# Splitting the last 16 rows off two loads of a batched matmul, and moving one operand mix to VectorE

## The chip, the cores and the metric

One core of a Trainium2 chip. Times are device microseconds (us) of one execution. Medians come from three runs or more; ratios are over the fast runs of both kernels in the same rounds, so they are not quite the ratio of the medians quoted. The interval behind a ratio is its 95% interval.

## The reference

```python
# x, y: [8, 12, 512, 64] float32
def reference(x, y):
    return np.einsum('bhtc,bhsc->bhts', x, y).astype(np.float32)   # [8, 12, 512, 512]
```

96 independent products of 512x64 by 64x512. The inputs are 25.17 MB, the output 100.66 MB, so this is a problem of transfers.

## The kernel before

Heads are taken in 12 load groups of 8. x of a group is one transfer of 128 rows of 8 KB into the left half of a "slot" (128 partitions x 16 KB), y of the group another into its right half. The five slots also hold the outputs on their way out. All transfers are issued by SyncE into one queue. `P` = 128, `Q` = 16, `R` = 32, `C` = 64, `NG` = 12, `SLOTS` = 5.

```python
    def slot():
        return slots.tile([P, K * S], fp32, name="slot")

    def load(g):
        both = slot()
        nc.sync.dma_start(both[:, :R * C], xv[g])
        nc.sync.dma_start(both[:, R * C:], yv[g])
        loaded[g] = both

    def compress(g):                  # float32 -> bf16; frees the slot
        both = loaded.pop(g)
        xk = kept.tile([P, R, C], bf16)
        nc.scalar.activation(xk..., both[:, :R * C], COPY)          # all of x, ScalarE
        ...
        # y in quarters: partitions 0-63 on VectorE and GpSimd (yb0),
        #                partitions 64-127 on VectorE and ScalarE (yb1)

    def mix(i, engines, halves=(0, 1)):    # xk into the zeroed operand tile, four copies
        ...

    def result(o):
        ...                                # matmuls into PSUM, two copies into a slot
        if h == 0 and i + 2 < 2 * NG:
            transposes(i + 2)
        elif h == 1 and FIRST <= i + 4 < 2 * NG:
            mix(i + 4, [nc.scalar if o % 4 == 3 else nc.vector] * 4)
        return lambda: nc.sync.dma_start(ov[i, h], otf)              # 2 MB store

    with tc.manual_schedule():
        for g in range(SLOTS):
            load(g)
        for half, engine, part in ((0, nc.vector, 256), (1, nc.gpsimd, 64)):
            for k in range(0, K * E * D, part):
                engine.memset(zeroed[half][:, k:k + part], 0.0)
        stores = []
        for g in range(NG):
            compress(g)
            mix(g // 2, [nc.gpsimd] * 4, (g % 2,))
            if g in (2, 4):
                transposes(g // 2 - 1)
            if g < 5:
                load(g + SLOTS)
            elif g in (5, 7, 9):
                stores.append(result(len(stores)))
            elif g in (6, 8):
                load(g // 2 + 7)
        ...
```

Below, x3 is the x load of group 3, y10 the y load of group 10. The slots go round: x5 can be issued when group 0 has been converted, the first output takes group 5's slot, and the last pair (x11, y11) takes group 8's.

## Time and profile before

| | before |
|---|---|
| time, median (lowest to highest) | 301.92 us (301.58 to 302.05, 5 runs) |
| span of the profiled run | 300.3 us |
| x0 landed, first to last of its 16 parts | 5.32 to 5.65 us |
| y2 landed | 17.73 to 18.05 us |
| x11 issued / landed | 54.19 / 59.98 to 60.29 us |
| last store's last part | 299.42 us |

One more row of the same page, what the transfers moved in each of the 40 slices (7.5 us each):

```profile
GB/s 282 430 422 421 420 423 422 421 432 443 420 432 438 417 434 437 421 437 434 420 437 434 423 432 432 423 443 426 421 450 419 426 439 423 419 437 428 426 434 194
```

From the second slice to the last but one the rate stays between 417 and 450 GB/s. Nothing that is lost in the queue of transfers can be won back later.

### The profile page before, as it was taken

What the parts mean: (1) busy time and instruction counts of PE and PEld (TensorE: products, weight loads), DVE (VectorE), ACT (ScalarE), POOL (GpSimd) and SP (SyncE); (2) the same over time, 40 slices, a digit from 0 to 9 for tenths busy, and PEclk for the clock granted to TensorE, in tenths of its full rate; (3) what the DMA queues carried; (4) which work ended last, traced back from release to release, by engine and by line L of the source; (5) the groups of instructions that cost most, each with busy time, mean ns of one, the idle gap of its engine ahead of it and who ended that gap; (6) DMA issues with size and microseconds to landing.
All of it is one profiled execution on the core that took longest, in us unless ns stands there. A gap on an engine that the chain in (4) does not pass through costs nothing.

```text
span 300.3 us, 1359 instructions
## 1 busy us (share of the span) xinstructions
PE 143.4 (48%) x384; PEld 46.3 (15%) x384; DVE 180.8 (60%) x136; ACT 219.2 (73%) x133; POOL 59.3 (20%) x56
## 2 busy tenths in 40 slices
PE   0004044037547674656675557664665675674000
PEld 0001011012212121211221112121221221121000
DVE  1568895969794973947909649289195552503200
ACT  4666599996999969789788697887887977364000
POOL 2899999991000000000000000000000000000000
PEclk9999995676998769767657866759667758577555
DMA  7999999999999999999999999999999999999994
GB/s 282 430 422 421 420 423 422 421 432 443 420 432 438 417 434 437 421 437 434 420 437 434 423 432 432 423 443 426 421 450 419 426 439 423 419 437 428 426 434 194
DMA packets 10375, 125.92 MB, mean 419 GB/s; under 512 B 1152, under 2 KB 1152, under 8 KB 1152
## 3 DMA queue, kind: packets, MB, share of 16 engines
q1 hardware_dynamic: 10368, 125.83, 98.8%
q8 instruction: 3, 0.05, 0.1%
q14 instruction: 4, 0.03, 0.0%
HBM read 25.17 MB, written 100.66 MB: 419 GB/s over the span
## 4 chain that ended last, share of the span: by engine, by line
DMA 49%; ACT 13%; DVE 5%; issue 4%; PE 1%; DVEq 1%; ACTq 0%
DMA out_dram<-slot 49%; ACT slot L65 10%; DVE slot L67 4%; ACT xb L65 2%; PE pm L134 1%; DVEq L191 1%; ACT xk L82 1%; DVE yb L67 0%; ACT yb L65 0%; DVE yT L120 0%; DVEq L67 0%; ACTq L65 0%
## 5 line engine op out<-in xcount | busy, mean ns | idle before, releaser
L134 PE MATMUL pm<-yT,xT 128*128 128x512 bf16 x384 | 143.4, 519 | 132.5 <-ACT slot L65 78.1
L65 ACT ACTIVATE slot<-pm 128x2048 f32<-128x2048 f32 x72 | 131.1, 1876 | 40.0 <-DMA out_dram<-slot 31.6
L67 DVE COPY slot<-pm 128x2048 f32<-128x2048 f32 x24 | 53.8, 2285 | 70.3 <-DMA out_dram<-slot 49.0
L134 PEld LDWEIGHTS <-xT 128*128 128x128 bf16 x384 | 46.3, 121 | 228.6 <-issue 192.6
L115 DVE STREAM_TRANSPOSE xT<-xb 128x1024 uint32<-128x1024 uint32 x24 | 49.1, 2044 | 8.4 <-PE pm L134 7.0
L65 ACT ACTIVATE xb<-xk 32x1024 bf16<-32x1024 bf16 x36 | 48.1, 1337 | 0.8
L67 DVE CAST yb<-slot 64x1024 bf16<-64x1024 f32 x24 | 32.7, 1362 | 19.0 <-DMA slot<-in_y_dram 18.7
L67 POOL COPY xb<-xk 32x1024 bf16<-32x1024 bf16 x24 | 38.1, 1589 | 1.2
L82 ACT ACTIVATE xk<-slot 128x2048 bf16<-128x2048 f32 x12 | 22.9, 1910 | 9.6 <-DMA slot<-in_x_dram 9.5
L67 DVE COPY xb<-xk 32x1024 bf16<-32x1024 bf16 x36 | 26.1, 725 | 0.4
L120 DVE STREAM_TRANSPOSE yT<-yb 128x512 uint32<-128x512 uint32 x24 | 25.2, 1048 | 0.0
L67 POOL CAST yb<-slot 64x1024 bf16<-64x1024 f32 x12 | 19.8, 1653 | 7.4 <-DMA slot<-in_y_dram 6.8
L65 ACT ACTIVATE yb<-slot 64x1024 bf16<-64x1024 f32 x12 | 15.9, 1328 | 3.6 <-DMA slot<-in_y_dram 3.4
L82 ACT ACT_TABLE_LOAD x1 | 1.3, 1283 | 0.7 <-PEq L180 0.7
L149 DVE MEMSET xb<- 128x256 uint32 x4 | 1.1, 272 | 0.9 <-PEq L180 0.9
L149 POOL MEMSET xb<- 128x64 uint32 x16 | 1.4, 152 | 0.3 <-POOLq L180 0.3
L180 POOL MEMSET const-float32-0.0<- 128x1 f32 x1 | 0.1, 98 | 0.2 <-issue 0.2
L180 POOL MEMSET const-float32-1.0<- 128x1 f32 x1 | 0.1, 98 | 0.0
L180 POOL MEMSET const-bfloat16-1.0<- 128x1 bf16 x1 | 0.1, 98 | 0.0
L180 POOL MEMSET const-uint8-127<- 128x1 uint8 x1 | 0.1, 98 | 0.0
## 6 DMA issues: line engine op xcount, KB each, us to landing
out_dram<-slot SPq DMA_DIRECT2D x48, 2048.0 KB, 20.5
slot<-in_x_dram SPq DMA_DIRECT2D x12, 1024.0 KB, 17.6
slot<-in_y_dram SPq DMA_DIRECT2D x12, 1024.0 KB, 19.3
```

The lines of the kernel that those rows point to most:

```text
L65: nc.scalar.activation(dst, src, COPY)
L67: engine.tensor_copy(dst, src)
L82: nc.scalar.activation(xk.rearrange("p r c -> p (r c)"), both[:, :R * C], COPY)
L115: nc.vector.transpose(xT.rearrange("p (k r e) -> p k e r", k=K, e=E), xb.rearrange("p (k e c) -> p k e c", k=K, e=E),)
L120: nc.vector.transpose(yT.rearrange("p (r j) -> p j r", r=D), yb.rearrange("p (j c) -> p j c", c=D))
L134: nc.tensor.matmul(pm[:, j, :], xT[:, k + j, h, :], yT[:, h * S:(h + 1) * S], start=True, stop=True)
L149: engine.memset(zeroed[half][:, k:k + part], 0.0)
L180: nc = _bacc.Bacc("TRN2", target_bir_lowering=False, num_devices=1)
L191: with _tile.TileContext(nc) as tc:
```

## The change

The intent, as far as the diff tells it: the 16 transfer engines don't end together (the last store's parts land over 3 us), so work is shifted between them. Of x0 and y2, only 112 rows go as one transfer; the last 16 rows go as four transfers of 4 rows, one behind each of the loads that follow. Two smaller edits: the last mix goes from ScalarE to VectorE, and a memset is done in one piece.

```diff
+    loaded, inputs, mixed, made, later = {}, {}, {}, {}, []
     def load(g):
+
         both = slot()
-        nc.sync.dma_start(both[:, :R * C], xv[g])
-        nc.sync.dma_start(both[:, R * C:], yv[g])
+        for src, dst, apart in ((xv[g], both[:, :R * C], g == 0), (yv[g], both[:, R * C:], g == 2)):
+            rows = P - Q if apart else P
+            nc.sync.dma_start(dst[:rows], src[:rows])
+            later.extend((dst[k:k + 4], src[k:k + 4]) for k in range(rows, P, 4))
+            if later:
+                nc.sync.dma_start(*later.pop(0))
         loaded[g] = both
@@ result
-            mix(i + 4, [nc.scalar if o % 4 == 3 else nc.vector] * 4)
+            mix(i + 4, [nc.scalar if o % 4 == 3 and i + 5 < 2 * NG else nc.vector] * 4)
@@ schedule
-        for half, engine, part in ((0, nc.vector, 256), (1, nc.gpsimd, 64)):
+        for half, engine, part in ((0, nc.vector, 1024), (1, nc.gpsimd, 64)):
```

The queue then holds, in order (s is a transfer of 4 rows): x0 (112 rows), s, y0, s, x1, s, y1, s, x2, y2 (112 rows), s, x3, s, y3, s, x4, s, y4, and so on with whole loads. x0 is complete with the fourth s, y2 with the eighth.

More of the change, by code (lines that the diff above doesn't have):

```diff
@@ L56 @@
     pmpool = ctx.enter_context(tc.tile_pool(name="pmpsum", bufs=2, space=bass.MemoryType.PSUM))
-    loaded, inputs, mixed, made = {}, {}, {}, {}
+    loaded, inputs, mixed, made, later = {}, {}, {}, {}, []
     zeroed = [const.tile([P, K * E * D], u32, name=f"xb{half}") for half in range(2)]
```

## The prediction

> **What bounds the kernel now.** I read the page from its second part down. First the row of the 40 slices, to see whether one resource is full all the time:
>
> ```profile
> PE   0004044037547674656675557664665675674000
> DVE  1568895969794973947909649289195552503200
> ACT  4666599996999969789788697887887977364000
> POOL 2899999991000000000000000000000000000000
> DMA  7999999999999999999999999999999999999994
> ...
> HBM read 25.17 MB, written 100.66 MB: 419 GB/s over the span
> ```
>
> The transfers are at 90% or more in every slice but the first and the last. No compute engine is full for long, except GpSimd (POOL) in the first quarter. The split by stage, cut where the loads end (62.7 us), says the same; its last two columns are the share of the transfer engines and GB/s:
>
> ```profile
> 57.50:62.70 5.20, 3.26 (x8) 1.04 (x8) 3.04 (x3) 5.16 (x3) 5.03 (x4) 0.54 1.03 427
> 62.70:150.00 87.30, 50.57 (x148) 16.87 (x147) 67.04 (x52) 75.94 (x48) 5.32 (x4) 0.78 1.01 431
> 150.00:296.00 146.00, 79.21 (x206) 25.08 (x204) 71.56 (x51) 97.11 (x59) 0.00 (x0) 0.67 1.01 429
> ```
>
> So the end is set by the queue of transfers: it must never run empty, and its 16 engines should end together. Two numbers come from the trace's record of when each of a transfer's 16 parts landed. The first load's parts land at 5.32 to 5.65 us, the eighth's at 22.70 to 23.03: 2.48 us a load of 128 rows, so **0.31 us a row** on each engine (8 rows). And the last store's parts land at 296.21 to 296.71 (twelve), 297.2, 297.2, 297.85 and **299.42**: one transfer engine ends 1.6 us after the next and 3 us after most. That is what the change seems to aim at.
>
> Then the early timeline, since there the change acts (start, length, engine, line, what; in brackets the idle time before it):
>
> ```profile
> 5.68 1.91 ACT L82 ACTIVATE xk<-slot 128x2048 bf16<-128x2048 f32 x1 [3.66 <-DMA slot<-in_x_dram]
> ...
> 10.09 3.07 POOL L67 COPY xb<-xk 32x1024 bf16<-32x1024 bf16 x2
> ...
> 20.58 2.02 DVE L115 STREAM_TRANSPOSE xT<-xb 128x1024 uint32<-128x1024 uint32 x1
> ...
> 33.25 3.52 DVE L67 CAST yb<-slot 64x1024 bf16<-64x1024 f32 x2
> ...
> 36.89 3.65 ACT L65 ACTIVATE slot<-pm 128x2048 f32<-128x2048 f32 x2 [2.58 <-DVE yb L67]
> ...
> 50.86 1.91 ACT L82 ACTIVATE xk<-slot 128x2048 bf16<-128x2048 f32 x1
> 52.80 1.32 ACT L65 ACTIVATE yb<-slot 64x1024 bf16<-64x1024 f32 x1
> ...
> 54.19 0.33 SPq L74 DMA_DIRECT2D slot<-in_x_dram  x1
> ```
>
> The reader is to see a chain: the first output copy (36.89) waits until VectorE has read y of load group 5, since it takes that group's buffer. From it ScalarE runs in order, without a gap worth naming, to its read of y of group 8 (ends 54.12), and only then is the last x load issued (54.19), into group 8's buffer. That load lands at 60.29, straight behind the one before it (57.79), so the queue never ran dry. How much slack is there? The first load, which found the queue empty, landed 4.9 us after issue (0.74 to 5.65). Issued at 54.19 onto an empty queue the last x load would have landed at 59.1. **The slack is 1.2 us.**
>
> [...] The trace before has only 128-row loads, each landing in 16 parts[...] all 24 loads land in the order of issue, 2.48 us apart. [...] One engine here moves 8 KB in 0.31 us, about 26 GB/s[...].
>
> **The change, part by part.**
>
> Rows moved: the two thinned loads lose 16 rows each, 1 row per engine and load if evenly, so all engines save 2 rows (0.62 us)[...] That is the whole gain on offer.
>
> When x of group 0 is complete: its last 4 rows stand behind y of group 1, the fourth load, which landed at 12.76 to 13.09. [...] 7+1+8+1+8+1+8+1 = 35 rows in place of 32, so it is 3 x 0.31 = 0.93 later: about **14.0 us, not 5.65**. The order of instructions shows the waits for these rows ahead of ScalarE's table load (1.28 us), so the first conversion of x runs from 15.2 to 17.1 and GpSimd's first pair of copies starts there instead of at 10.09. GpSimd is then 7 us late, with about 4.8 us of work per group against 4.97 us per group of loads: it recovers almost nothing.
>
> When y of group 2 is complete: its last 4 rows stand behind x of group 4, the ninth load (25.18 to 25.51). [...] 78 rows there in place of 72: 6 x 0.31 = 1.86 later, **27.4 us, not 18.05**. Its lower 64 partitions are needed by VectorE and GpSimd only from the 112 rows, so GpSimd is not held again; but VectorE's and ScalarE's casts of the upper half wait, and both run in order.
>
> VectorE from 27.4, with the durations of before: second half of y2 1.24 (28.6); the transpose pair 2.8 (31.4); y3 2.5 (33.9); y4 2.5 (36.4); the next transpose pair 2.8 (39.2; GpSimd's copies for it end near 34.8); y5 2.5 to 3.5 (about **42.2**; before 36.77). The first output copy on ScalarE starts there. Before, from that copy to the issue of the last x load it was 54.19 - 36.89 = 17.3 us, all ScalarE's own work in order; I keep it. VectorE's casts of y7, needed for the second output copy, end near 52.3 (GpSimd to 44.5, transposes 2.8, two groups of casts 5.0), just in time for 52.5. So the last x load is issued at 42.2 + 17.3 = **59.5**, and lands at 59.5 + 4.9 = 64.4 instead of 60.29. **The queue runs empty and the loads end 4.1 us later.** After it the stores have their lead back: the fourth store can be issued near 74.3 and is due only near 81, so nothing is added. Nor is it won back, as the queue is full from there to the end. The empty queue also lines the engines up again: [...] so the 0.62 us gain is lost.
>
> The last x mix: four ScalarE copies of 1.337 us (5.3) become four of VectorE's 0.725 us (2.9), late in the store phase where both have idle time: 0. One memset of 1024 columns for four of 256 (0.272 each, 1.1 in all): 0, since it ends long before the first y lands. Eight more issues on SyncE at some 0.33 to 0.65 us each fit under 2.5 us of transfer per load: 0.
>
> Sum: 301.92 + 4.1 = **306.0 us**.
>
> **The rivals.** (a) The balancing works and no hole opens: 301.92 - 0.6 = 301.3. For it: the 3 us of imbalance at the end, and a change so particular that its author may have measured it. Against it: 1.2 us of slack against a delay of 5.3 us. [...] (b) [...] a small transfer takes 4 to 5 row times, 1.2 to 1.5 us instead of 0.31, [...] some 8 us more at y of group 2. VectorE's chain moves with it, and the last x load, with earlier ones, comes about 9 us later still: 306 + 9 = 315. [...] partial overlap would give 308 to 311. (c) ScalarE or GpSimd becomes the bound for good: GpSimd has work only to 68 us, and later stores have leads of 20 us from issue to landing, so no.
>
> **Range and chances.** I give (a) a quarter, the hole alone (303 to 308) a little over a third, (b) in part or in full the rest. Two per cent slower is 308.0, so slower gets 0.41, same 0.58; a gain of over 2% (below 295.9) is under the transfers' own time, 0.01. The range 300.9 to 315.0 covers (a) to nearly all of (b).
>
> **What would show it.** Right: the first conversion of x starts near 15 us; the casts of y of group 2 end near 29; the last x load is issued near 59.5; the slices of the transfers show a dip near 57 to 62 us with ScalarE's wait or SyncE's wait on ScalarE's y cast ahead of it. Wrong: no dip and the last load landing near 60 (then (a)); or small transfers that land over a microsecond after the load ahead of them, and dips already near 38 us (then (b)).

## The result, and the profile after

The changed kernel took **317.72 us** (317.39 to 318.39, 5 runs) against 301.92: ratio 1.0531 [1.0516, 1.0545], slower. 306.0 and a range of 300.9 to 315.0 had been predicted. The profiled spans differ by 16.0 us (316.3 against 300.3).

The page of the changed kernel, its second and third part (tenths of busy time in 40 slices of 7.9 us, then the rate):

```profile
DVE  1312299995998767296592955919569195501400
ACT  0065294999799997896988878888788547285000
POOL 1229699993600000000000000000000000000000
...
DMA  7999999959999999999999999999999999999995
GB/s 218 334 258 314 335 423 421 400 218 311 431 429 430 432 431 431 431 429 430 431 431 431 431 431 425 431 431 431 431 433 429 431 431 429 423 433 427 431 429 222
...
HBM read 25.17 MB, written 100.66 MB: 398 GB/s over the span
```

The row of busy transfers shows one dip, in the ninth slice. The row of rates shows two losses: slices 2 to 5 (7.9 to 39.5 us) run at 258 to 335 GB/s **while the engines count as busy**, and slices 8 to 10 hold the dip. The same in a split by stage; the last two columns are the share of the transfer engines and GB/s. Before:

```profile
3.00:28.00 25.00, 3.57 (x8) 1.24 (x9) 13.60 (x10) 14.85 (x9) 19.16 (x12) 1.00 1.01 424
57.00:80.00 23.00, 11.86 (x35) 4.03 (x35) 19.05 (x16) 20.25 (x13) 10.85 (x7) 0.74 1.02 432
```

After, and a second split of it around the dip:

```profile
3.00:28.00 25.00, 0.00 (x0) 0.00 (x0) 5.76 (x5) 9.66 (x6) 8.13 (x6) 1.00 1.01 298
57.00:80.00 23.00, 8.98 (x20) 2.65 (x19) 19.22 (x13) 22.62 (x14) 16.90 (x12) 0.50 0.81 304
```

```profile
69.00:71.40 2.40, 0.00 (x0) 0.00 (x0) 2.37 (x2) 2.35 (x3) 2.14 (x2) 0.50 0.01 3
```

From 3 to 28 us the share is 1.01 in both kernels, but the rate is 298 in place of 424 GB/s. So in this trace the share doesn't tell the loss and the rate does: an engine whose row is held up (the next table has rows of up to 1299 ns) counts as busy. From 69.0 to 71.4 us the queue was truly empty (3 GB/s).

What the rows themselves took, from the trace's record of each row's transfer, 3.3 to 28 us, 8 KB rows only:

| kernel | rows over 350 ns | rows over 700 ns, number | longest |
|---|---|---|---|
| before | 0.1% | 0 | 460 ns |
| after | 45% | 82 | 1299 ns |

It begins with the 112 rows of x0 by themselves: of the rows that started between 3.3 and 5.2 us, before any part of a small transfer had landed (the first at 6.58), 65 of 69 took over 350 ns, against 1 of 99 in the kernel before. The 112 rows of y2 (21.0 to 24.0 us) had a median of 572 ns a row, where a row took 0.31 us before. And between 9.1 and 10.45 us, around the second small transfer, **all 16 engines** had a row of 0.78 us or more (the trace names no engine, but 16 such rows are in flight at once from 9.75 to 9.95 us).

The timeline of the changed kernel (start, length, engine, line, what; in brackets the idle time before it), to be read beside the prediction's:

```profile
18.20 1.28 ACT L87 ACT_TABLE_LOAD   x1 [18.20 <-DMA slot<-in_x_dram]
19.49 1.91 ACT L87 ACTIVATE xk<-slot 128x2048 bf16<-128x2048 f32 x1
...
21.46 2.68 POOL L67 COPY xb<-xk 32x1024 bf16<-32x1024 bf16 x2 [8.98 <-ACT xk L87]
...
37.25 1.33 ACT L65 ACTIVATE yb<-slot 64x1024 bf16<-64x1024 f32 x1 [9.28 <-DMA slot<-in_y_dram]
37.25 0.72 DVE L67 CAST yb<-slot 64x1024 bf16<-64x1024 f32 x1 [9.89 <-DMA slot<-in_y_dram]
...
49.49 3.54 DVE L67 CAST yb<-slot 64x1024 bf16<-64x1024 f32 x2
...
53.15 3.65 ACT L65 ACTIVATE slot<-pm 128x2048 f32<-128x2048 f32 x2 [4.69 <-DVE yb L67]
...
69.05 1.33 ACT L65 ACTIVATE yb<-slot 64x1024 bf16<-64x1024 f32 x1
...
70.44 0.33 SPq L77 DMA_DIRECT2D slot<-in_x_dram  x1
...
79.41 2.49 DVE L67 CAST yb<-slot 64x1024 bf16<-64x1024 f32 x2 [3.58 <-DMA slot<-in_y_dram]
```

The first conversion of x starts at 19.49 and not at 5.68; VectorE and ScalarE wait 9.9 and 9.3 us for the last rows of y2; the first output copy starts at 53.15 and not at 36.89; x11 is issued at 70.44 and not at 54.19.

Where the 16 us were lost is told by the landing times of the last loads (last of the 16 parts, from the trace's own record):

| | before | after | later by | added in this step |
|---|---|---|---|---|
| y10 (22nd load) | 57.79 | 69.03 | 11.24 | 11.24 |
| x11 (behind the dip) | 60.29 | 75.34 | 15.05 | 3.81 |
| y11 | 63.35 | 79.38 | 16.03 | 0.98 |
| last store | 299.42 | 315.43 | 16.01 | -0.02 |

So 11.2 us were lost in the slow stretch, 3.8 in the empty queue, and 1.0 at the hand-over from loads to stores. Of y10's parts twelve are 9.8 to 10.0 us late and four 11.2 (as many as the parts of a small transfer); six more rows on these four, at 0.31 us (the prediction's estimate: 78 rows in place of 72), are 1.9 of these 11.2, and the rest is slow rows. The stores took the same time in both. The last store's parts again land in the pattern of before: twelve at 312.46 to 312.92, then 313.88, 314.14, 314.39 and 315.43. Nothing was balanced.

### The profile page after: what moved, and what is told of

It reads as the page before. It is cut to its first block, busy times and chain, and to the rows that moved or that the text cites.

```text
span 316.3 us, 1370 instructions
## 1 busy us (share of the span) xinstructions
PE 143.4 (45%) x384; PEld 46.2 (15%) x384; DVE 186.6 (59%) x137; ACT 214.1 (68%) x129; POOL 56.4 (18%) x56
## 4 chain that ended last, share of the span: by engine, by line
DMA 44%; ACT 15%; DVE 4%; issue 4%; PE 3%; DVEq 1%; ACTq 0%
DMA out_dram<-slot 44%; ACT slot L65 12%; DVE slot L67 4%; PE pm L139 3%; ACT xb L65 1%; ACT yb L65 1%; DVEq L196 1%; ACT xk L87 1%; DVE yb L67 0%; DVE yT L125 0%; DVEq L67 0%; ACTq L65 0%
## 5 line engine op out<-in xcount | busy, mean ns | idle before, releaser
L67 DVE CAST yb<-slot 64x1024 bf16<-64x1024 f32 x24 | 35.5, 1480 | 33.4 <-DMA slot<-in_y_dram 33.1
L65 ACT ACTIVATE xb<-xk 32x1024 bf16<-32x1024 bf16 x32 | 42.8, 1337 | 0.7
L67 POOL COPY xb<-xk 32x1024 bf16<-32x1024 bf16 x24 | 37.2, 1551 | 11.0 <-ACT xk L87 9.0
L67 DVE COPY xb<-xk 32x1024 bf16<-32x1024 bf16 x40 | 29.0, 726 | 0.4
L65 ACT ACTIVATE yb<-slot 64x1024 bf16<-64x1024 f32 x12 | 15.9, 1329 | 9.6 <-DMA slot<-in_y_dram 9.3
L67 POOL CAST yb<-slot 64x1024 bf16<-64x1024 f32 x12 | 17.8, 1487 | 16.5 <-DMA slot<-in_y_dram 16.0
L154 DVE MEMSET xb<- 128x1024 uint32 x1 | 0.9, 912 | 1.0 <-PEq L185 1.0
```

The costliest lines, as they stand in the source:

```text
L65: nc.scalar.activation(dst, src, COPY)
L67: engine.tensor_copy(dst, src)
```

## The experiments

Three theories stood at first. **PLACE**: whether rows collide, that is, hold up each other and the rows of the loads, depends on the partitions that they go to; rows of neighbouring ones do (an assumption). **COUNT**: a transfer of few rows costs its time wherever it goes. **LATE**: the cost is that rows arrive late, behind other loads. The figures that the expectations of e2, e4, e5, e6 and e10 give first are those of PLACE. In each case the time is that of the run named, against 301.7 to 302.0 for the kernel before on the same chip.

### 1. The two other edits alone (e1)

The changed kernel with whole loads; the memset and the last mix stay changed.

```diff
-        for src, dst, apart in (...):          # the split
-            ...
+        nc.sync.dma_start(both[:, :R * C], xv[g])
+        nc.sync.dma_start(both[:, R * C:], yv[g])
```

> The changed kernel with its loads put back whole (128 rows, no 4-row transfers); the single memset and VectorE's last x mix stay. All theories: the loads alone are to blame, so 301.9 us within 0.5 of the kernel before. If the other two edits cost or gain anything, it shows here.

Measured: 302.18 us, ratio 1.0009 [0.9994, 1.0024]. The two edits are worth nothing; all 15.8 us come from the split loads.

### 2. The same 16 rows in one piece (e6), and the small ones straight behind their load (e7)

```diff
 e6:
-            later.extend(...)
-            if later:
-                nc.sync.dma_start(*later.pop(0))
+            if apart:
+                nc.sync.dma_start(dst[rows:], src[rows:])
 e7:
-            if later:
+            while later:
                 nc.sync.dma_start(*later.pop(0))
```

> The changed kernel, but the last 16 rows of x 0 and y 2 go in one 16-row transfer straight behind the 112 rows: no 4-row transfers, no late completion. [...] rows of the 112-row transfers still collide ([...]0.45 to 0.65 us a row), and the 16 rows[...] take about 1.1 us; together 5 to 6 us of stall, about 307 us unless slack hides it nowhere, as the queue is always full. Rival (only the 4-row transfers and the lateness are to blame): 302 us.

> The changed kernel, but the four small transfers stand straight behind their 112 rows, so x 0 is complete near 11 us and y 2 near 26 us counted with all collisions before it. All collisions stay, the lateness goes. If the two causes add (collisions delay the loads by about 10 us, lateness adds the empty queue of about 5 us): 311.5 us, with no empty stretch before the last x load. If lateness is no cause of its own: 317.7 us.

Measured: e6 306.09 us (1.0138 [1.0123, 1.0153]); e7 311.36 us (1.0315 [1.0291, 1.0339]). Both close to what was expected (some 307 and 311.5). In both, x0 and y2 are completed right behind their 112 rows (e7: y2 at 28.59 us, against 37.23 in the changed kernel), so little of LATE is left. The splits by stage, e6 and then e7:

```profile
3.00:28.00 25.00, 0.26 (x1) 0.21 (x2) 10.54 (x9) 13.20 (x9) 14.74 (x10) 1.00 1.01 356
```

```profile
3.00:28.00 25.00, 0.00 (x0) 0.00 (x0) 5.62 (x5) 9.67 (x6) 12.73 (x8) 1.00 1.02 283
57.00:80.00 23.00, 7.31 (x17) 2.25 (x17) 16.04 (x13) 20.68 (x13) 20.27 (x13) 0.50 0.98 383
```

e7 has the slow stretch of the changed kernel (283 GB/s) but hardly its dip: the share from 57 to 80 us is 0.98 in place of 0.81. By the medians, and roughly, slow transfers cost 311.36 - 301.96 = 9.4 us, and having the rows behind later loads 317.72 - 311.36 = 6.4. The cut costs 4 us even when its 16 rows go in one piece (e6).

### 3. Extra small transfers beside whole loads (e4, e5, e10)

To have the small transfers by themselves: the kernel before, with eight extra transfers of 4 rows x 5.6 KB into a tile that nobody reads, at the places in the queue where the changed kernel has them. e4 takes four neighbouring partitions of 96 to 127; e5 takes partitions 4 apart, 16 in a span, from the same region; e10 takes partitions 0, 4, 8, 12 and so on from 0 to 15 and 32 to 47. In the changed kernel each small transfer landed in four parts; by estimate, eight of them here give four of the engines eight short rows more each.

```diff
+    spare = const.tile([P, 1408], fp32, name="spare")
+    # later: at eight places, which partitions
+    #   e4:  lo + 4*j .. lo + 4*j + 3      with lo = 112, then 96
+    #   e5:  lo + j, +4, +8, +12           with lo = 112, then 96
+    #   e10: lo + j, +4, +8, +12           with lo = 0, then 32
+            if (g, which) in later:
+                some = later[g, which]
+                nc.sync.dma_start(spare[some], src[g][some, :1408])
```

> The kernel before, all loads whole, plus eight extra 4-row transfers (5.6 KB a row, 4 neighbouring partitions each) into an unused tile, behind the loads where the change has its own. No 112-row transfer, nothing completes late. [...] each holds up all engines for some 0.5 to 0.7 us (four rows[...] at 0.21 us a row alone), so the tenth load lands 4 to 5.5 us late and the time is 305 to 308 us. Rival: small neighbouring transfers are harmless without the 112-row ones or the lateness: 302 to 303 us.

> The same, with the extra transfers' rows 4 partitions apart. [...] the tenth load lands 1 to 2.5 us late and the time is 302 to 304.5 us, clearly under the run with neighbouring rows. Rival COUNT (fixed cost per transfer): the same as with neighbouring rows.

> The eight extra 4-row transfers again, into partitions 0, 4, 8, 12 and their like[...] no row of the first 10 loads takes longer than 0.35 us; [...] 8 x 0.21 = 1.7 us more, the others nothing; if the engine that ends last is not among them, 302.0 us, else 303.6. Rival COUNT (each small transfer stalls all engines, wherever its rows go): 305.5 us, as with the other two placings.

| | time, ratio [95%] | rows over 350 ns / number over 700 ns | y10 landed, first to last part (before: 57.49 to 57.79) |
|---|---|---|---|
| e4 | 306.38, 1.0137 [1.0114, 1.0161] | 18% / 48 | 61.14 to 62.85 |
| e5 | 305.48, 1.0118 [1.0101, 1.0134] | 20% / 7 | 59.52 to 62.11 |
| e10 | 303.43, 1.0056 [1.0039, 1.0073] | 0.2% / 0 | 57.59 to 59.37 |

The splits by stage of e4, e5 and e10:

```profile
3.00:28.00 25.00, 1.92 (x5) 0.80 (x6) 11.23 (x10) 12.64 (x8) 15.49 (x10) 1.00 1.01 369
```

```profile
3.00:28.00 25.00, 1.81 (x5) 0.80 (x6) 11.56 (x10) 12.94 (x8) 15.82 (x10) 1.00 1.01 389
```

```profile
3.00:28.00 25.00, 3.57 (x8) 1.24 (x9) 12.70 (x10) 14.07 (x9) 18.16 (x12) 1.00 1.01 424
```

The same eight transfers, the same bytes at the same places in the queue: with four neighbours of 96 to 127 the first part of y10 is 3.65 us late, in e10 0.1 us. So **COUNT falls**: the number of transfers and their size are the same, and which rows they take decides. PLACE fits. Why those rows and not others was not shown: the trace names no engine and not which partition a row goes to, and the rows that are read from HBM changed together with the partitions that are written, so a cause on the reading side was not ruled out. e5 misses its expectation of 302 to 304.5 us: its rows, 4 apart in the region of e4, leave 20% of the rows over 350 ns (e4 18%), though fewer over 700 ns (7 against 48), and the times of e4 and e5 are not clear of each other. e10's rows are 4 apart as well, and 0.2% are over 350 ns. So it is not the distance between the rows by itself that decides.

One thing more stands in these traces: the small rows themselves took 0.22 us in all three kernels. The slow ones are 8 KB rows of the loads, and in e4 210 of the 224 slow rows between 3.3 and 40 us started within 1 us after a small row.

In e10 twelve engines are 0.1 us late at y10 and four 1.6 us, close to 8 x 0.22 us for rows of 5.6 KB. The cost of 4-row transfers that I had predicted is thus right for the rows of e10. e10 still loses 1.6 us by the medians; the first parts of x11 are 0.15 us late and those of y11 1.35, so nearly all of it comes between these two. See experiment 6.

### 4. The split rows of the real loads, 4 apart (e2)

```diff
-            later.extend((dst[k:k + 4], src[k:k + 4]) for k in range(rows, P, 4))
+            later.extend((dst[k:P:4], src[k:P:4]) for k in range(rows, rows + (4 if apart else 0)))
```

> The changed kernel, but each 4-row transfer takes rows 4 apart (112+j, 116+j, 120+j, 124+j) in place of 4 neighbouring ones: same count, size, order, waits. [...] rows of the small transfers take 0.31 to 0.65 us in place of 1.1, only the two 112-row transfers stay slow (some 4 us together) and the late completion of x 0 and y 2 stays; about 309 us, range 305 to 312. Rival COUNT (a transfer on 4 engines costs a fixed stall whatever its rows): unchanged, 317.7 us.

Measured: 314.26 us (313.36 to 315.28), 1.041 [1.0377, 1.0442]. Outside the expected 305 to 312, between the two expectations: spreading the rows wins 3.5 of 15.8 us. That is in line with e5, where rows 4 apart left 7 rows over 700 ns against 48 in e4, though about as many over 350 ns (20% against 18%). The 112-row part, which e6 shows to be slow as well (y2's rows took a median of 468 ns there, in place of 310), is unchanged.

### 5. Late whole loads, nothing split (e3, e8, e9)

The kernel before, with only the order of the first ten loads changed. e8 has y2 ninth, e9 has x0 fourth, e3 both.

```diff
-            load(g)
+            loaded[g] = slot()
+        # e3: y0 x1 y1 x0 x2 x3 y3 x4 y2 y4
+        # e8: x0 y0 x1 y1 x2 x3 y3 x4 y2 y4
+        # e9: y0 x1 y1 x0 x2 y2 x3 y3 x4 y4
+        for g, which in (...):
+            load_one(g, which)
```

> The kernel before with whole loads, but issued in another order: x of group 0 fourth, y of group 2 ninth. No small and no 112-row transfer, only the late completion (x 0 lands near 13.1 us, y 2 near 25.5). Theory LATE (my predicted chain): VectorE's casts of y 5 end near 41.1 in place of 36.8, the last x load is issued near 58.4 and lands near 63.3 in place of 60.3: 304.9 us. If lateness is harmless (all the loss is in the transfers themselves): 301.9 us.

> Whole loads, x 0 first as in the kernel before, y of group 2 ninth. By my chain the lateness of y 2 drives VectorE's order and with it the last x load: nearly all of the 6.9 us that both late loads cost, 307 to 309 us. If the lateness of x 0 (GpSimd's start) is what counts: 302 to 303 us.

> Whole loads, x of group 0 fourth (lands near 13.1 us), y of group 2 in its usual turn. As y 2 alone cost 6.9 us, and both together no more, x 0 alone should cost nothing that y 2 did not hide: VectorE's first transposes wait for GpSimd by a microsecond or two at most and the last x load has 1.2 us of slack: 302 to 303.5 us. Rival (any late first load empties the queue later): 305 us or more.

| | time, ratio [95%] | first output copy | x11 issued | x11 / y11 landed, against before |
|---|---|---|---|---|
| before | 301.92 | 36.89 | 54.19 | |
| e9 (x0 late) | 304.79, 1.0098 [1.0083, 1.0113] | 38.89 | 57.39 | +1.88 / +2.92 |
| e8 (y2 late) | 308.79, 1.0227 [1.0211, 1.0242] | 44.16 | 61.45 | +5.90 / +6.89 |
| e3 (both) | 308.84, 1.0232 [1.0215, 1.025] | 44.21 | 61.52 | +6.00 / +6.95 |

Here no row is slow in the first 50 us (from 3.3 to 28 us at most 3 of some 1280 rows over 350 ns); the split by stage of e3:

```profile
3.00:28.00 25.00, 0.00 (x0) 0.00 (x0) 6.36 (x6) 10.84 (x7) 10.59 (x8) 1.00 1.01 424
```

424 GB/s, as before, and yet 6.9 us are lost: 6.0 by the time x11 lands, and 1.0 behind it. Of the 6.0, 0.9 are there when y10 lands, as x10 was issued at 51.20 in place of 43.88; the rest is an empty queue ahead of x11. The row of rates of e8 shows the gap in its seventh to ninth slice:

```profile
GB/s 292 427 421 424 419 424 375 224 265 434 435 419 440 424 427 438 423 438 431 424 438 433 425 433 427 433 431 425 440 429 427 435 427 431 425 429 431 431 425 226
```

So LATE is a true cost of its own. e8 came as expected (307 to 309), but e3 missed its 304.9: right in kind, and 3.9 us too small. e8's timeline shows part of the reason:

```profile
25.46 2.48 DVE L67 CAST yb<-slot 64x1024 bf16<-64x1024 f32 x2 [9.96 <-DMA slot<-in_y_dram]
...
30.70 7.07 DVE L67 CAST yb<-slot 64x1024 bf16<-64x1024 f32 x4
...
31.93 3.51 POOL L67 COPY xb<-xk 32x1024 bf16<-32x1024 bf16 x2
...
40.52 3.52 DVE L67 CAST yb<-slot 64x1024 bf16<-64x1024 f32 x2
...
44.16 3.65 ACT L65 ACTIVATE slot<-pm 128x2048 f32<-128x2048 f32 x2 [7.48 <-DVE yb L67]
...
61.45 0.33 SPq L74 DMA_DIRECT2D slot<-in_x_dram  x1
```

A pair of VectorE casts took 2.48 us in the first place and 3.5 us in the next ones, where GpSimd's mix copies ran at the same time (that they slow each other down fits, and was not tested by itself). The four casts of y3 and y4 took 7.07 us where I had counted 5.0. From the first output copy to the issue of x11 it is 17.29 us (44.16 to 61.45), the 17.3 of before.

e9 missed too (302 to 303.5 expected): a late x0 holds GpSimd's copies up, and the first output copy then waits for GpSimd's cast of y5, no longer for VectorE's:

```profile
12.99 1.91 ACT L85 ACTIVATE xk<-slot 128x2048 bf16<-128x2048 f32 x1 [10.98 <-DMA slot<-in_x_dram]
...
38.89 3.65 ACT L65 ACTIVATE slot<-pm 128x2048 f32<-128x2048 f32 x2 [4.66 <-POOL yb L67]
...
57.39 0.33 SPq L74 DMA_DIRECT2D slot<-in_x_dram  x1
```

Both late together cost as much as y2 alone: the later of two waits counts, not their sum (308.84 us against 308.79).

### 6. What stays between x11 and y11

In the kernel before the first part of y11 lands 2.48 us behind the first part of x11. In the changed kernel it is 3.64, in e3 3.70, in e8 3.60, in e9 3.53, in e10 3.68; in ten of the fourteen kernels it is 2.7 to 3.7. The table above has the same: from x11 to y11 another 1.0 us is lost in e3, e8 and e9. In e10 there was no empty queue, but four engines were 1.6 us behind; in e8 there was an empty queue, and all engines were in step. Both show it, so neither is needed for it, and no run tested what is. **It stays open.** The traces show two things about it. The rows of y11 are slow themselves: in e8 82 of the 112 rows recorded from the first landing of x11 to the last of y11 took over 350 ns, in the kernel before 1 of 105. So whole loads can have slow rows too, which PLACE doesn't explain. And over all fourteen kernels the loss goes with the time from x11's issue to its first landing: 5.6 to 5.9 us where y11 loses at most 0.1 (before, e1, e11, e12), 4.9 in e6 (0.2 lost), 4.7 in e4 (0.7), and 4.2 to 4.5 in the other eight (1.0 to 1.3). Nothing was run to vary this by itself. It accounts for 1.0 of e9's 2.9 us (the other 1.9 are the late x11) and most of e10's 1.6.

### 7. The aim itself: free one engine at the end (e11, e12)

The last store's parts end up to 3 us apart. If that is one engine that ends late, a last store that goes in fewer parts might spare it. The kernel before, with the last store in two pieces: 120 and 8 rows (e11) or 112 and 16 (e12).

```diff
+        def store():
+            cut = 60 if o == 4 * NG - 1 else 64          # e12: 56
+            nc.sync.dma_start(ov[i, h][:cut], otf[:2 * cut])
+            if cut < 64:
+                nc.sync.dma_start(ov[i, h][cut:], otf[2 * cut:])
+        return store
```

> An attempt at the aim of the change, without touching the loads: the kernel before, but its last store goes as 120 rows (15 engines, 8 rows each) and 8 rows (4 engines, 2 each), which frees one engine of the last store's 8 rows. The engine that ends last is 1.6 us behind the next. If it is the freed one and reads of neighbouring partitions do not collide: about 300.4 us. If another one: 301.9. If reads collide as the writes of the 112-row loads did: 303 to 306 us.

> The same with 112 rows (14 engines, 8 rows each) and 16 rows (8 engines, 2 each), which frees two engines. If the last engine is one of these two and reads do not collide: 300.4 us, the other engines' 1.2 us more still end sooner. If another one: 301.9 to 302.5. If reads collide: 303 to 306 us.

Measured: e11 305.43 us (1.0118 [1.0103, 1.0133]), e12 305.58 us (1.013 [1.0113, 1.0147]). Slower by some 3.8 and 3.9 us, within the 303 to 306 us expected if reads collide. At the end of the run 81 (e11) and 77 (e12) rows took over 0.7 us, half of them 1.0 to 1.3, in place of 0.61. The pieces landed in 15 and 4 parts (e11), 14 and 8 (e12), as expected. So stores, which read the on-chip memory, are held up by such a cut too. Which engine ends last stays open, and no version here beats the kernel before.

## Why the prediction was wrong

**Step 1, the size of a small transfer, failed.** It said "7+1+8+1+8+1+8+1 = 35 rows in place of 32, so it is 3 x 0.31 = 0.93 later: about 14.0 us". Measured: the four small ones of x0 landed at 7.24, 10.86, 14.48 and 18.11 us, one every 3.62 us, which is 2.48 for the load ahead and **1.14 for the small one**, not 0.31. And not for the engines of its four parts alone: all 16 were held up. y2 was complete at 37.23 and not at 27.4. Two terms were missing in the sum: what a small transfer costs the other rows, depending on where it goes (e4 against e10), and the 112-row transfers, which I took as one row an engine less at the same 0.31 us a row, and whose rows were slow from the start, before any small transfer (65 of 69 over 350 ns). The eight small ones, each 0.83 us dearer than predicted, would make 6.6 of the 9.8 us by which y2 was later than predicted, and the 112-row pieces the rest (an estimate). The cut with its 16 rows in one piece cost 4 us (e6). Why rows of the 112-row pieces are slow was not shown, and which rows an engine gets was not seen in any run.

Around the second small transfer, which landed in four parts at 10.24 to 10.86 us, all 16 engines had a row of 0.78 us or more within 1.35 us. How a transfer in four parts holds up the other engines, no run shows.

**Step 2, VectorE's chain from y2 to the first output copy, was nearly right.** 14.8 us predicted (27.4 to 42.2), 15.9 measured (37.23 to 53.15). The excess is of the kind seen in e8: casts of 3.5 us a pair beside GpSimd's copies. The kernel before had such pairs too (3.52 us at 33.25, among the prediction's own lines), so the 2.5 taken for y3 and y4 was too short a reading.

**Step 3, from that copy to the issue of x11, was right:** 17.3 predicted, 70.44 - 53.15 = 17.29 measured. (ScalarE is fuller in this stretch than the prediction's first reading says: in the kernel before its row stands at 9 in eight of the slices 6 to 14.)

**Step 4, from issue to landing on an empty queue, was right:** 4.9 predicted, 75.34 - 70.44 = 4.90 measured. The empty queue cost 3.8 us against 4.1 predicted. But that agreement is partly luck: both ends of the hole moved. The loads ahead of it were themselves 11.2 us late, and x11 was 11 us later than predicted.

**Step 5 was right but for the hand-over.** No balance was won at the end, as the empty queue lined the engines up again: the parts of y10, ahead of it, landed over 1.78 us (67.25 to 69.03), those of x11, behind it, over 0.58 us (74.76 to 75.34). "Nothing is added" after the last load is true of the stores (-0.02 us), but y11 itself cost 1.0 us more. The prediction had read all 24 loads as 2.48 us apart; in the kernel before, the last part of y11 already came 3.06 us behind that of x11.

**Step 6 was right.** The last mix and the memset are worth nothing (e1: 1.0009).

Set out as one sum: 306.0 had 4.1 for the hole; the runs show 3.8 for it, plus **11.2 for late loads ahead of it** (slow rows but for at most 1.9) and 1.0 at the hand-over, 16.0 in all. Along the prediction's own chain it is 4.1, plus 9.8 because y2 was complete later (step 1), 1.1 for VectorE (step 2) and 1.0 for y11. Rival (b) had named the kind of loss: a small transfer of several row times (1.2 to 1.5 us there, 1.14 measured) and a landing "over a microsecond after the load ahead" (1.4 us from the fourth small one on). It fell short in size: it has some 8 us more at y2, where 9.8 were measured, and no term for the 112-row pieces.

## What to carry to other kernels

Splitting a few rows off a load that covers all 128 partitions can cost far more than their bytes, in this kernel 1.1 us for 32 KB and on all engines; which rows the small transfer takes decides (e4 against e10). Why those rows and not others was not shown. Look for it in the rate and in the time of single rows, since the busy share stays at 1.0 (1.01 here at 298 and at 424 GB/s). And before a load is moved back in the queue, follow the chain from its consumer to the next issue: here some 0.6 us of balance was on offer, by the prediction's estimate, and having the rows late cost about 6.4.
